# The output projection as seven block products instead of eight, with precomputed weight sums

## The chip, the core and the metric

The kernel runs on one core of a Trainium2 chip. The core has TensorE (PE, matrix products, with its weight loads shown apart as PEld), VectorE (DVE), ScalarE (ACT), GpSimd (POOL) and SyncE (SP, which here only issues DMAs). The engines run side by side, each through its own queue in order, and wait for one another through semaphores. The metric is the device time of one execution in microseconds, the median of several runs; each change is compared with the kernel before on the same chip.

## What is computed

One layer of a generator backbone: a modulated RMSNorm, a combined input projection, three groups of heads (a short convolution, neighbourhood attention, a conformer convolution), an output projection with a gated residual, and a last RMSNorm. Cut to what matters here, with x of 1024 rows and 1024 columns:

```python
mod = jax.nn.silu(c) @ w_ada[l] + b_ada[l]
shift, scale, gate = jnp.split(mod, 3, axis=-1)
...
ya = short_conv_branch(zl[0], zl[1], zl[2], zl[3], conv_sc[l])
yb = neighbourhood_attention(heads(zl[4]), heads(zl[5]), heads(zl[6]), kc, vc, rpb[l])
yb = yb * jax.nn.silu(zl[7])
yc = conformer_branch(zl[8], zl[9], zl[10], conv_cf[l], conv_cf_b[l], ln_cf_g[l], ln_cf_b[l])
y = jnp.concatenate([ya, yb, yc], axis=-1) @ w_out[l]
x = x + gate[:, None, :] * y
return rmsnorm(x, final_g)
```

Everything is float32. The product with `w_out` is 1024 x 1024 by 1024 x 1024.

## The kernel before

Matrix products are made in a rounded format: each float32 operand is split into a high part (a copy on ACT, line 129) and a low part (the difference, line 130, on DVE or on POOL), and a product is three matmuls: high by high, high by low, low by high. All y is kept transposed: eight channel tiles `y[0..7]` of 128 channels by 1024 positions; 0 and 1 come from the short convolution, 2 to 5 from attention, 6 and 7 from the conformer branch. Tiles 0 to 5 are written to DRAM (`yd`) when they are made and loaded again for the output projection.

The kernel first normalises and projects (up to about 150 us), then runs attention over four pairs of heads (`attend`, `attention`). There, for each block of 128 queries, PE makes scores (lines 596 and 597), DVE adds the bias and takes a minimum (601), ACT takes the exponential (604), POOL scales (606), PE transposes (615), ACT and DVE split (619, 620) and PE multiplies with the values (627). Other projections (329 to 331) and background work fill the gaps: a coroutine that is started with `spawn` emits a step whenever PE's estimated time has gone on by the gap that it yields, and `after_pe` puts an instruction behind the matmul emitted last, in the planner's order only. PE's order is the order in which the code emits; the orders of DVE, ACT, POOL and SP in this part are chosen by a planner when the program is built, and are then fixed queues.

The output stage follows attention (from line 1133). `load_wout(0)` loads and splits the left half of `w_out`, `load_y` loads and splits y; `cf_out` makes the last two y tiles with 96 projection matmuls; then come the products. `out_mm` makes one tile of 128 positions by 512 columns from all eight channel tiles, tile by tile, for the left half of the columns and then for the right: 8 tiles, 2 halves, 8 channels, 3 matmuls, that is 384 matmuls of 512 columns (the last tile's half in two pieces of 256). The first four tiles take channels 2 to 7 first and 0 and 1 behind the gate (`gate_rows`). For each tile and half, `out_part` (887) adds the gated result to the residual `xres` on DVE and sums squares on ACT (905); the left half is multiplied by the gate on DVE (894, 895), while for the right half the gate has been multiplied into the weights on POOL (865). `out_gain` (909) multiplies the first finished half by the last norm's gain on POOL, `out_mean` and `out_scale` work out the norm's factor on POOL (915 to 928) and scale on ACT (931) and DVE (933, 935), and each half is stored.

## Time and profile before

| | us |
|---|---|
| median of 3 runs (607.11 to 607.23) | 607.14 |
| the profiled execution | 607.07 |
| its span, from the first to the last instruction | 605.3 |
| first matmul of the output projection | 509.5 |
| start of its last matmul | 598.75 |
| end of DVE's last instruction | 601.55 |

The granted clock of TensorE was 0.997 of full speed in the mean. HBM traffic was 55.93 MB read and 14.29 MB written. Times in a profile are microseconds from the start of the span. A row of a timeline gives the start, the duration, the engine, the line, the operation, what it writes and reads, and in brackets the idle time before it and who ended it. A row of groups gives the count, the busy time, the mean duration in ns and the idle time before. Matmuls overlap one another: what a matmul costs is the distance between starts, not its own duration.

### The profile page before, as it was taken

What the parts mean: (1) busy time and instruction counts of PE and PEld (TensorE: products, weight loads), DVE (VectorE), ACT (ScalarE), POOL (GpSimd) and SP (SyncE); (2) the same over time, 40 slices, a digit from 0 to 9 for tenths busy, and PEclk for the clock granted to TensorE, in tenths of its full rate; (3) what the DMA queues carried; (4) which work ended last, traced back from release to release, by engine and by line L of the source; (5) the groups of instructions that cost most, each with busy time, mean ns of one, the idle gap of its engine ahead of it and who ended that gap; (6) DMA issues with size and microseconds to landing.
All of it is one profiled execution on the core that took longest, in us unless ns stands there. A gap on an engine that the chain in (4) does not pass through costs nothing.

```text
span 605.3 us, 8913 instructions
## 1 busy us (share of the span) xinstructions
PE 587.7 (97%) x3101; PEld 493.2 (81%) x3101; DVE 400.1 (66%) x681; ACT 245.9 (41%) x470; POOL 182.8 (30%) x194
## 2 busy tenths in 40 slices
PE   7799999999999999999999999999999999999995
PEld 4467888888898988888888988888887888888885
DVE  4466988665686699578897666936889347383222
ACT  2455721111355533454423555425655334024222
POOL 1031143000353212334112432114433460199311
PEclk9999999999999999999999999999999999999998
DMA  8992576975624026332145242172301464941122
GB/s 279 357 338 73 192 248 193 104 143 166 158 57 111 18 87 174 81 84 53 34 147 128 50 113 56 48 214 66 86 17 32 141 195 120 371 146 36 71 104 105
DMA packets 97170, 78.64 MB, mean 130 GB/s; under 512 B 26507, under 2 KB 80869, under 8 KB 96997
## 3 DMA queue, kind: packets, MB, share of 16 engines
q1 hardware_dynamic: 95397, 71.51, 42.6%
q10 hardware_dynamic: 1728, 6.55, 3.1%
q8 instruction: 25, 0.41, 0.3%
q14 instruction: 20, 0.16, 0.1%
HBM read 55.93 MB, written 14.29 MB: 116 GB/s over the span
## 4 chain that ended last, share of the span: by engine, by line
PE 86%; DVE 4%; ACT 3%; POOL 2%; issue 1%; DMA 1%; SPq 1%; POOLq 0%; DVEq 0%; ACTq 0%
PE ps_z L329 14%; PE ps_z L331 14%; PE ps_z L330 14%; PE po L627 5%; PE ps_t L615 5%; PE ps_f L878 5%; PE ps_f L879 5%; PE ps_f L877 5%; PE ps_s L596 3%; PE ps_z L419 3%; PE ps_z L421 3%; PE ps_z L420 3%; PE ps_s L597 2%; DMA wr<-in_w_in 1%; PE ps_h L279 1%
## 5 line engine op out<-in xcount | busy, mean ns | idle before, releaser
L329 PE MATMUL ps_z<-h,wh 128*128 128x512 f32 x384 | 151.1, 394 | 0.0
L331 PE MATMUL ps_z<-h,wl 128*128 128x512 f32 x384 | 150.3, 391 | 0.0
L330 PE MATMUL ps_z<-h,wh 128*128 128x512 f32 x384 | 149.8, 390 | 0.0
L130 POOL TENSOR_TENSOR wl<-wr,wh 128x512 fp32r<-128x512 f32 x44 | 61.4, 1399 | 165.4 <-ACT wh L129 162.0
L606 POOL TENSOR_SCALAR pr<-pr,sm 128x640 f32<-128x640 f32 (+1 forms) x64 | 56.6, 884 | 135.9 <-DVE sm L605 116.1
L331 PEld LDWEIGHTS ps_z<-h,wl 128*128 128x128 f32 x384 | 72.1, 188 | 16.1
L330 PEld LDWEIGHTS ps_z<-h,wh 128*128 128x128 f32 x384 | 72.1, 188 | 12.4
L329 PEld LDWEIGHTS ps_z<-h,wh 128*128 128x128 f32 x384 | 72.1, 188 | 12.1
L692 DVE SCALAR_TENSOR_TENSOR acc<-t,half_w,acc 128x1024 f32<-128x1024 f32 x60 | 80.6, 1343 | 1.2
L619 ACT ACTIVATE pw<-ps_t 128x640 fp32r<-128x640 f32 (+1 forms) x64 | 43.5, 680 | 86.8 <-PE ps_t L615 86.6
L601 DVE CUSTOM_DVE_ANT_0 ps_s<-ps_s,bt 128x640 f32<-128x640 f32 (+1 forms) x64 | 50.9, 796 | 27.1 <-PE ps_s L597 23.7
L620 DVE TENSOR_TENSOR pw<-ps_t,pw 128x640 fp32r<-128x640 f32 (+1 forms) x64 | 50.4, 788 | 15.8 <-ACT pw L619 15.5
L604 ACT ACTIVATE pr<-ps_s,mn 128x640 f32<-128x640 f32 (+1 forms) x64 | 49.1, 766 | 19.7 <-DVE mn L601 18.9
L878 PE MATMUL ps_f<-wol,y 128*128 128x512 f32 (+1 forms) x136 | 51.6, 379 | 0.0
L879 PE MATMUL ps_f<-woh,y 128*128 128x512 f32 (+1 forms) x136 | 51.6, 379 | 0.0
L877 PE MATMUL ps_f<-woh,y 128*128 128x512 f32 (+1 forms) x136 | 51.5, 379 | 0.0
L627 PE MATMUL po<-pw,vt 128*128 128x256 f32 x304 | 51.4, 298 | 0.0
L129 ACT ACTIVATE wh<-wr 128x512 fp32r<-128x512 f32 x46 | 29.0, 630 | 42.1 <-PE ps_z L330 21.7
L615 PE MATMUL ps_t<-ident,pr 128*128 128x128 f32 x304 | 43.6, 272 | 0.6 <-DVE sm L605 0.6
L596 PE MATMUL ps_s<-kt,qd 128*128 128x384 f32 (+1 forms) x128 | 39.8, 333 | 1.0 <-ACT pr L604 0.9
L627 PEld LDWEIGHTS po<-pw,vt 128*128 128x128 f32 x304 | 40.5, 190 | 0.3
L615 PEld LDWEIGHTS ps_t<-ident,pr 128*128 128x128 f32 x304 | 35.5, 141 | 2.1 <-issue 1.0
(169 smaller groups left out, 921.8 us busy)
## 6 DMA issues: line engine op xcount, KB each, us to landing
wr<-in_w_in SPq DMA_DIRECT2D x52, 256.0 KB
wa<-in_w_ada SPq DMA_DIRECT2D x16, 512.0 KB
qd<-qn SPq DMA_DIRECT2D x32, 256.0 KB
vd<-t SPq DMA_DIRECT2D x20, 256.0 KB
x_in<-in_x SPq DMA_DIRECT2D x8, 512.0 KB
t<-in_w_ada SPq DMA_DIRECT2D x16, 256.0 KB
vt<-vd SPq DMA_DIRECT2D x32, 128.0 KB
fraw<-in_w_out SPq DMA_DIRECT2D x8, 512.0 KB
```

Source lines behind the costliest of these rows:

```text
L130: i2 = (eng or nc.vector).tensor_tensor(out=lo, in0=src, in1=f32(hi), op=ALU.subtract)
L329: nc.tensor.matmul(ps, lhsT=wh, rhs=hh, start=(k == 0), stop=False)
L330: nc.tensor.matmul(ps, lhsT=wh, rhs=hl, start=False, stop=False)
L331: self.last = nc.tensor.matmul(ps, lhsT=wl, rhs=hh, start=False, stop=(k == KT - 1))
L596: nc.tensor.matmul(win, lhsT=q[:, b % 4], rhs=kwin, start=(i == 0), stop=(i == 1))
L606: nc.gpsimd.tensor_scalar(out=pr, in0=pr, scalar1=sm, scalar2=0.5, op0=ALU.mult, op1=ALU.mult)
L615: nc.tensor.transpose(out=pt[:, c * P:(c + 1) * P], in_=pr[:, c * P:(c + 1) * P], identity=self.ident)
L627: self.nc.tensor.matmul(po, lhsT=vt[:, vi, h], rhs=pw[:, c], start=(c == 0), stop=(c == n - 1))
L692: self.after_pe(nc.vector.scalar_tensor_tensor(out=acc, in0=u[:, t:t + T], scalar=self.half_w[:, 2 * t + ct:2 * t + ct + 1], in1=acc, op0= ...
L877: nc.tensor.matmul(ps, lhsT=yh, rhs=wh[:, ch], start=(first and i == 0), stop=False)
L878: nc.tensor.matmul(ps, lhsT=yh, rhs=wl[:, ch], start=False, stop=False)
L879: nc.tensor.matmul(ps, lhsT=yl, rhs=wh[:, ch], start=False, stop=(last and i == len(chs) - 1))
```

## The change

Write A for y (positions by channels) and B for `w_out`, each as 2 x 2 blocks of 512. The output blocks are made from seven block products. With S1 = A21 + A22, S2 = S1 - A11, S3 = A11 - A21, S4 = A12 - S2 and T1 = B12 - B11, T2 = B22 - T1, T3 = B22 - B12, T4 = T2 - B21, and with U = A11 B11 + S2 T2:

- left, first positions: A11 B11 + A12 B21
- right, first positions: U + S1 T1 + S4 B22
- left, second positions: U + S3 T3 - A22 T4
- right, second positions: U + S3 T3 + S1 T1

The sums T1 to T4 are made during attention by a new coroutine `out_weights` on POOL, split by ACT and POOL, in eight groups of [128 x 256] pieces, and written to DRAM (`wtd`, four tensors of 2.1 MB). The sums of y are made on DVE after `cf_out`; y is now kept unsplit and each A, S is split when it is needed (`y_parts`). Each product is `out_mm4`: four channel tiles outside, four position tiles inside, so four PSUM banks fill side by side and a quarter of the weights is free after every 12 matmuls; `load_wt` brings the next product's quarters into the same eight buffers. U and the sums on it are kept in SBUF tiles `fu`. Two sets of four PSUM banks take turns. The gate is now multiplied onto every result (`out_part` and two places beside it), partly on POOL (`G`); the weights no longer take it. The last product (A22 T4) goes tile by tile, the last tile in two pieces. `load_wout` and `y_tiles` go.

The diff, cut; lines of the old output loop are left out:

```diff
     def cf_out(self, ct):
         nc = self.nc
         acc, ch = self.acc_cf[ct], 6 + ct
-        yh, yl = self.y[ch] = self.y_tiles(ch, self.fp)
+        y = self.y[ch] = self.fp.tile([P, T], F32, name=f"y{ch}")
         def sink(half, ps):
             sl = slice(half * HALF, (half + 1) * HALF)
             sg = self.t2.tile([P, HALF], F32, name="t2", tag="t2")
             self.silu2(sg, ps)
-            nc.vector.scalar_tensor_tensor(out=sg, in0=acc[:, sl], scalar=0.25, in1=sg, op0=ALU.mult, op1=ALU.mult)
-            self.split(yh[:, sl], yl[:, sl], sg)
+            nc.vector.scalar_tensor_tensor(out=y[:, sl], in0=acc[:, sl], scalar=0.25, in1=sg, op0=ALU.mult, op1=ALU.mult)
...
+    def out_weights(self, pool, gap):
+        nc = self.nc
+        n = 256
+        for i in range(4):
+            for c in range(0, HALF, n):
+                def raw(k, half):
+                    t = pool.tile([P, n], F32, name="bg", bufs=5)
+                    nc.sync.dma_start(out=t, in_=self.a["w_out"][k * P:(k + 1) * P, half * HALF + c:half * HALF + c + n])
+                    return t
+                b11, b12, b21, b22 = raw(i, 0), raw(i, 1), raw(4 + i, 0), raw(4 + i, 1)
+                t1 = pool.tile([P, n], F32, name="bg", bufs=5)
+                yield gap
+                for name, out, x, y in (("T1", t1, b12, b11), ("T3", b12, b22, b12), ("T2", t1, b22, t1), ("T4", t1, t1, b21)):
+                    self.after_pe(nc.gpsimd.tensor_tensor(out=out, in0=x, in1=y, op=ALU.subtract))
+                    yield gap
+                    p = pool.tile([P, 2, n], F32R, name="bgp", bufs=2)
+                    i1, i2 = self.split(p[:, 0], p[:, 1], out, nc.gpsimd)
+                    self.after_pe(i1)
+                    self.after_pe(i2)
+                    yield gap
+                    nc.sync.dma_start(out=self.wtd[name][:, :, i, c:c + n], in_=f32(p))
+    def load_wt(self, name, pool):
+        w = [pool.tile([P, 2, HALF], F32R, name="wt", bufs=8) for _ in range(4)]
+        if name in self.wtd:
+            for i, t in enumerate(w):
+                self.nc.sync.dma_start(out=f32(t), in_=self.wtd[name][:, :, i])
+        return w
+    def load_b(self, pool, i, j, q, **kw):
+        src = self.a["w_out"][(4 * i + q) * P:(4 * i + q + 2) * P, j * HALF:(j + 1) * HALF]
+        t = pool.tile([P, 2, HALF], F32, **kw)
+        self.nc.sync.dma_start(out=t, in_=src.rearrange("(k p) n -> p k n", p=P))
+        return t
+    def split_b(self, w, raw, q):
+        for i in range(2):
+            self.split(w[q + i][:, 0], w[q + i][:, 1], raw[:, i], self.nc.gpsimd)
     def load_y(self, ch, pool):
-        raw = self.fr.tile([P, T], F32, name="fraw")
-        self.nc.sync.dma_start(out=raw, in_=self.yd[ch])
-        self.y[ch] = self.y_tiles(ch, pool)
-        self.split(*self.y[ch], raw)
+        self.y[ch] = pool.tile([P, T], F32, name=f"y{ch}")
+        self.nc.sync.dma_start(out=self.y[ch], in_=self.yd[ch])
...
+    def y_parts(self, pool, srcs):
+        r = []
+        for src in srcs:
+            t = pool.tile([P, 2, HALF], F32R, name="yc")
+            self.split(t[:, 0], t[:, 1], src)
+            r.append(t)
+        return r
...
+    def out_mm4(self, ps, y, w, first=True, skip=False):
+        for i in range(4):
+            for t in range(4):
+                self.out_mm(ps[t], i, t, y, w, first and i == 0, i == 3, skip=skip)
...
-    def out_part(self, tt, cs, j, ps, lp, eng):
+    def out_part(self, tt, cs, j, ps, lp, eng, op=ALU.add):
         nc = self.nc
         xt, ss = self.xres[tt]
         n = cs.stop - cs.start
         g = lp.tile([P, HALF], F32, name="fg", bufs=2)[:, 0:n]
-        if j == 0:
-            nc.vector.tensor_tensor(out=g, in0=ps[:, 0:n], in1=self.gate[:, cs], op=ALU.mult)
-            nc.vector.tensor_tensor(out=xt[:, cs], in0=g, in1=xt[:, cs], op=ALU.add)
-        else:
-
-            nc.vector.tensor_tensor(out=xt[:, cs], in0=ps[:, 0:n], in1=xt[:, cs], op=ALU.add)
+        nc.vector.tensor_tensor(out=g, in0=ps[:, 0:n], in1=self.gate[:, cs], op=ALU.mult)
+        nc.vector.tensor_tensor(out=xt[:, cs], in0=xt[:, cs], in1=g, op=op)
...
+        self.spawn(self.out_weights(r(self.pool("bg", 1, side="right")), 3.2), 4.0)
...
+            wt = e(self.pool("wt", 8, side="right"))
+            ya = e(self.pool("ya", 4, side="right"))
+            frs = ExitStack()
+            fr = frs.enter_context(self.pool("fr", 2, side="right"))
+            y, V, S, G = self.y, nc.vector, nc.scalar, nc.gpsimd
+            for ch in range(4):
+                self.load_y(ch, self.fp)
+            b11, b21 = (self.load_wt(n, wt) for n in ("B11", "B21"))
+            for i, b in enumerate((b11, b21)):
+                for q in (0, 2):
+                    self.split_b(b, self.load_b(fr, i, 0, q, name="fraw"), q)
+                if i == 0:
+                    a11 = self.y_parts(ya, [y[ch][:, 0:HALF] for ch in range(4)])
+            for ch in (4, 5):
                 self.load_y(ch, self.fp)
             self.run(self.cf_out(0), self.cf_out(1))
+            frs.close()
             inp.close()
             self.lp = lp = e(self.pool("lp", 1, side="left"))
...
+            ps_g = e(self.pool("ps_g", 4, PSUM, side="right"))
+            yc = e(self.pool("yc", 12, side="left"))
+            def banks(n=4, g=False):
+                pool, name, tag = (ps_g, "ps_g", "g") if g else (self.ps_f, "ps_f", "f")
+                return [pool.tile([P, HALF], F32, name=name, tag=tag) for _ in range(n)]
+            a12 = self.y_parts(yc, [y[4 + i][:, 0:HALF] for i in range(4)])
+            self.gate_load(lp, yc)
             self.fgam = lp.tile([P, D], F32, name="fgam")
             nc.scalar.dma_start(out=self.fgam, in_=self.a["final_g"].partition_broadcast(P))
...
             self.xres = []
...
+            sync, act = nc.sync.dma_start, nc.scalar.dma_start
+            h0, h1 = slice(0, HALF), slice(HALF, D)
+            u = []
+            ps = banks()
+            self.out_mm4(ps, a11, b11, skip=True)
+            for t in range(4):
+                u.append(lp.tile([P, HALF], F32, name=f"fu{t}"))
+                S.activation(out=u[t], in_=ps[t], func=AF.Copy)
+            for tt in range(4):
+                self.out_tile(tt, lp)
+            self.gate_rows(ps_g)
+            s1 = []
+            for i in range(4):
+                s = lp.tile([P, HALF], F32, name=f"fs{i}")
+                k1, k2 = y[i], y[4 + i]
+                V.tensor_tensor(out=s, in0=k1[:, h1], in1=k2[:, h1], op=ALU.add)
+                V.tensor_tensor(out=k1[:, h1], in0=k1[:, h0], in1=k1[:, h1], op=ALU.subtract)
+                V.tensor_tensor(out=k1[:, h0], in0=s, in1=k1[:, h0], op=ALU.subtract)
+                V.tensor_tensor(out=k2[:, h0], in0=k2[:, h0], in1=k1[:, h0], op=ALU.subtract)
+                s1.append(s)
+            t2 = self.load_wt("T2", wt)
+            s2 = self.y_parts(yc, [y[i][:, h0] for i in range(4)])
+            self.out_mm4(ps, a12, b21, False, skip=True)
+            t1 = self.load_wt("T1", wt)
+            s1 = self.y_parts(yc, s1)
+            raw = [self.load_b(yc, 1, 1, q, name="yc") for q in (0, 2)]
+            for t in range(4):
+                self.out_part(t, h0, 0, ps[t], lp, S)
+                self.out_mean(t, 0)
+                self.out_gain(t, h0)
+            ps = banks(g=True)
+            self.out_mm4(ps, s2, t2)
+            t3 = self.load_wt("T3", wt)
+            s3 = self.y_parts(yc, [y[i][:, h1] for i in range(4)])
+            for t in range(4):
+                V.tensor_tensor(out=u[t], in0=ps[t], in1=u[t], op=ALU.add)
+            for tt in range(4, 8):
+                self.out_tile(tt, lp)
+            ps = banks()
+            self.out_mm4(ps, s1, t1)
+            b22 = self.load_wt("B22", wt)
+            for q in (0, 2):
+                self.split_b(b22, raw[q // 2], q)
+            s4 = self.y_parts(yc, [y[4 + i][:, h0] for i in range(4)])
+            for t in range(4):
+                v = lp.tile([P, HALF], F32, name="fv", bufs=2)
+                V.tensor_tensor(out=v, in0=ps[t], in1=u[t], op=ALU.add)
+                V.tensor_tensor(out=v, in0=v, in1=self.gate[:, h1], op=ALU.mult)
+                for tt, eng in ((t + 4, V), (t, G)):
+                    x = self.xres[tt][0][:, h1]
+                    eng.tensor_tensor(out=x, in0=x, in1=v, op=ALU.add)
+            ps = banks(g=True)
+            self.out_mm4(ps, s3, t3)
+            t4 = self.load_wt("T4", wt)
+            a22 = self.y_parts(yc, [y[4 + i][:, h1] for i in range(4)])
+            for t in range(4):
+                V.tensor_tensor(out=u[t], in0=ps[t], in1=u[t], op=ALU.add)
+                self.out_part(t + 4, h1, 0, ps[t], lp, S)
+                self.out_mean(t + 4, 0)
+                G.tensor_tensor(out=u[t], in0=u[t], in1=self.gate[:, h0], op=ALU.mult)
+                x = self.xres[t + 4][0][:, h0]
+                G.tensor_tensor(out=x, in0=x, in1=u[t], op=ALU.add)
+                self.out_gain(t + 4, h1)
+            ps = banks()
+            self.out_mm4(ps, s4, b22)
+            for t in range(4):
+                self.out_part(t, h1, 1, ps[t], lp, S)
+                self.out_scale(t, 1, ((h0, S, sync), (h1, None, sync)))
+            ps = banks(3, True)
+            for t in range(3):
+                for i in range(4):
+                    self.out_mm(ps[t], i, t, a22, t4, i == 0, i == 3)
+                self.out_part(t + 4, h0, 1, ps[t], lp, S, ALU.subtract)
+                self.out_scale(t + 4, 1, ((h1, S, sync), (h0, None, sync)))
+            ps = banks(2)
+            q = [slice(c, c + 256) for c in (0, 256)]
+            for j in range(2):
+                for i in range(4):
+                    self.out_mm(ps[j], i, 3, a22, t4, i == 0, i == 3, 256 * j, 256 * j + 256)
+                self.out_part(7, q[j], 1 + j, ps[j], lp, (S, V)[j], ALU.subtract)
+                if j == 0:
+                    self.out_gain(7, q[0])
+                    self.out_mean(7, 1)
+            self.out_scale(7, 2, ((h1, S, act), (q[0], V, None), (q[1], None, sync)))
```

83 lines of the change are left out of this document (13 added, 70 removed).

## The prediction

> **What bounds the kernel now.** The page comes first, for the span, the busy shares and the chain of work that ended last.
>
> ```profile
> span 605.3 us, 8913 instructions
> PE 587.7 (97%) x3101; PEld 493.2 (81%) x3101; DVE 400.1 (66%) x681; ACT 245.9 (41%) x470; POOL 182.8 (30%) x194
> PE 86%; DVE 4%; ACT 3%; POOL 2%; issue 1%; DMA 1%; SPq 1%; POOLq 0%; DVEq 0%; ACTq 0%
> ```
>
> TensorE is busy for 97% of the span and carries 86% of the chain. The waits of PE from 150 to 480 us, which is all of attention, come next; these three rows are the whole answer.
>
> ```profile
> PE ps_z L734 <- DVE t L724: 1.0, 2, 0.7
> PE ps_s L596 <- ACT pr L604: 0.9, 3, 0.5
> PE ps_t L615 <- DVE sm L605: 0.6, 1, 0.6
> ```
>
> PE waits 2.5 us there in all. Then the table by stretches, over the output stage (columns: length, then busy time and count of PE, PEld, DVE, ACT, POOL; clock, DMA share, GB/s).
>
> ```profile
> 480.00:509.00 29.00, 29.00 (x129) 24.01 (x129) 14.51 (x15) 12.38 (x17) 12.51 (x6) 1.00 0.58 179
> 509.00:526.00 17.00, 17.00 (x77) 14.03 (x76) 6.34 (x9) 3.65 (x5) 0.00 (x0) 1.00 0.76 269
> 526.00:554.00 28.00, 28.00 (x125) 23.07 (x124) 18.65 (x16) 8.97 (x18) 25.43 (x14) 1.00 0.44 151
> 554.00:575.00 21.00, 21.00 (x92) 16.94 (x91) 5.72 (x8) 5.07 (x11) 11.15 (x17) 1.00 0.14 51
> 575.00:599.00 24.00, 24.00 (x128) 20.29 (x126) 6.12 (x9) 6.31 (x14) 4.25 (x10) 1.00 0.29 110
> ```
>
> From 509 to 599 PE never stops and DVE works 18.65 of 28 us at its worst and a quarter of the time later (6.12 of 24). So this stage is PE's: a matmul less is a matmul's time less, as long as the other engines keep up. Whether they do is the whole question.
>
> **What is removed.** The view of tile ps_f gives the matmuls of the output projection, the PE timeline the start of the last one.
>
> ```profile
> L877 PE MATMUL ps_f<-woh,y x136: 276/389/398, 509.5 to 598.5; 128*128 128x512 f32 x120, 128*128 128x256 f32 x16
> 525.89 1.09 PE L843 MATMUL ps_g<-ghl,ones_r 128*128 128x512 f32 x4
> 526.82 0.39 PE L877 MATMUL ps_f<-woh,y 128*128 128x512 f32 x1
> 598.75 0.28 PE L879 MATMUL ps_f<-woh,y 128*128 128x256 f32 x1
> ```
>
> Three lines of 120 full and 16 half matmuls are 384 full ones. They take 598.75 - 509.5 less the 0.93 us of the gate matmuls (525.89 to 526.82): 88.3 us, or 0.230 us each. Seven products of 4 x 4 x 3 are 336. PE saves 48 x 0.230 = **11.0 us**, and its last matmul would start near 587.7. The multiplication by the gate of the second weight half on POOL (L865) goes too; it hid behind PE.
>
> **What is added after cf_out.** The DVE and POOL timelines have the prices, and what the two do to each other.
>
> ```profile
> 510.91 0.58 ACT L390 ACTIVATE t<-ps_z 128x512 f32<-128x512 f32 x1
> 512.36 0.69 DVE L802 SCALAR_TENSOR_TENSOR t<-acc,t 128x512 f32<-128x512 f32 x1
> 528.39 0.69 DVE L894 TENSOR_TENSOR fg<-ps_f,gate 128x512 f32<-128x512 f32 x1 [0.55 <-PE ps_f L879]
> 531.66 2.17 DVE L895 TENSOR_TENSOR xres<-fg,xres 128x512 f32<-128x512 f32 x1
> 533.76 0.68 DVE L894 TENSOR_TENSOR fg<-ps_f,gate 128x512 f32<-128x512 f32 x1
> 540.16 1.34 DVE L895 TENSOR_TENSOR xres<-fg,xres 128x512 f32<-128x512 f32 x1
> 555.07 0.69 DVE L895 TENSOR_TENSOR xres<-fg,xres 128x512 f32<-128x512 f32 x1
> 595.99 0.75 DVE L935 SCALAR_TENSOR_TENSOR xres<-xres,fss,fgam 128x512 f32<-128x512 f32 x1 [1.85 <-POOL fss L928]
> 596.66 0.42 DVE L898 TENSOR_TENSOR xres<-ps_f,xres 128x256 f32<-128x256 f32 x1
> 601.07 0.48 DVE L935 SCALAR_TENSOR_TENSOR xres<-xres,fss,fgam 128x256 f32<-128x256 f32 x1
> 528.06 5.22 POOL L865 TENSOR_TENSOR fraw<-fraw,gate 128x1024 f32<-128x1024 f32 x2 [32.36 <-DVE gate L845]
> 533.25 5.73 POOL L130 TENSOR_TENSOR wol<-fraw,woh 128x1024 fp32r<-128x1024 f32 x2
> 539.66 1.29 POOL L909 TENSOR_TENSOR xres<-xres,fgam 128x512 f32<-128x512 f32 x1
> L895 DVE TENSOR_TENSOR xres<-fg,xres 128x512 f32<-128x512 f32 x8 | 13.6, 1697 | 0.3
> ```
>
> An independent DVE instruction starts about 0.08 us before its forerunner's record ends (595.99 + 0.75 against 596.66), so a full [128 x 512] one costs 0.61 us of DVE and a scaling 0.67. DVE can begin the new work when cf_out's last values are made; the last of them was ready at 512.36 + 0.69. Its tanh (L390) started at 510.91 though its matmuls ended by 509.5, because ACT copied for a split that is now gone; 1.4 us earlier, and with the overlap of 0.08, is 511.5. From the diff, DVE then has, full width: two SBUF inputs: 16 sums of y, 24 splits (a12, s2, s1, s3, s4, a22), 4 residual additions after the second product, 8 after the fourth, 4 + 4 + 3 after the last three, 63 in all; one PSUM input: 2 for the gate and 4 + 4 + 4 + 8 + 4 + 3 evictions, 29; 7 scalings; and about 2.9 us on the last tile's halves. That is 92 x 0.61 + 7 x 0.67 + 2.9 = **63.7 us**. Before, DVE was busy 18.65 + 5.72 + 6.12 = 30.5 us from 526 to 599.
>
> To this come the waits for POOL. L895, two SBUF inputs, takes 0.69 us when POOL rests (555.07), 1.34 when it meets a 1.29 us POOL instruction (540.16) and 2.17 when it meets 2.6 us ones. It ends half a microsecond after POOL's instruction does (531.66 + 2.17 = 533.83; POOL's pair ended at 533.28), while L894, which reads PSUM, stays at 0.69. So the two take turns: a DVE instruction with two SBUF inputs waits out POOL's. The row of 540.16 prices a meeting with a 512-wide one at 1.34 - 0.69 = 0.65 us, and POOL now has little else than those.
>
> The Trainium skill (SBUF — State Buffer, section "SBUF: two separate sides") calls this port pair an exclusive lock that the first comer holds for its whole instruction, with no sharing of bandwidth; the ends quoted above agree. By sharing instead, each meeting would cost what the group's mean shows, 1.70 - 0.69 = 1.01 us, and the waits worked out below would come to 33 us, not 21.
>
> How many meetings? These rows price POOL's small steps.
>
> ```profile
> 563.50 0.27 POOL L925 TENSOR_SCALAR fss<-fss 128x1 f32<-128x1 f32 x1
> 563.85 0.56 POOL L928 TENSOR_TENSOR fss<-fss,mhalf 128x1 f32<-128x1 f32 x1
> 597.76 0.74 POOL L909 TENSOR_TENSOR xres<-xres,fgam 128x256 f32<-128x256 f32 x1 [1.80 <-ACT fsq L905]
> ```
>
> POOL after 511.5: about 3 splits left of B21, 4 of B22, 8 gains (0.74 us of them narrow), 12 sums into u and the residual, near 27 x 1.29 + 0.74 = 35.6 us, and some 9 us of small steps (8 x 0.83 and the means): 45 us. Over a stage of 95 us that is 0.47 of the time. DVE's 63 + 7 instructions with two SBUF inputs then wait 70 x 0.47 x 0.65 = **21 us** (none if the two always miss each other; 70 x 0.65 = 45 if every one meets one, as most of L895's eight do with their mean of 1.70). Bunching speaks for more: in the fifth product POOL gets four 512-wide instructions for one tile of evictions less one, 3 x 1.29 + 0.3 = 4.2 us a tile, 17 us in all against a product of 48 x 0.230 = 11.0 us. Everything it does for the last norms (L925, L928) stands behind that backlog.
>
> ```profile
> 508.93 0.68 DVE L391 SCALAR_TENSOR_TENSOR t<-t,ps_z 128x512 f32<-128x512 f32 x1
> 509.65 0.69 DVE L802 SCALAR_TENSOR_TENSOR t<-acc,t 128x512 f32<-128x512 f32 x1
> 573.64 0.75 DVE L935 SCALAR_TENSOR_TENSOR xres<-xres,fss,fgam 128x512 f32<-128x512 f32 x1 [1.85 <-POOL fss L928]
> 515.25 9.80 ACTq L883 DMA_DIRECT2D xres<-in_x  x4
> ```
>
> Idle time of DVE: some 27 pairs in which it reads its own last result (509.65 follows 508.93 + 0.68 by 0.04 where independent ones overlap 0.08, so 0.12 each, 3 us), and waits at the end for POOL's small steps behind the backlog. Before, such a wait was 1.85 us a tile. I take **8 us**, between 4 (one wait) and 14 (six).
>
> ACT has room: 28 copies for splits, 8 for B21 and B22, 4 of u at near 0.6 us, and the norms as before, some 40 us of 90. But its queue also issues the residual loads, and four took 9.80 us to issue. The copies of u, which free the banks for the second product, and the split copies stand behind them. That delay is 0 to 9.8 us of PE; I take 0 for the end, since DVE is already late there. DMA adds 8.4 MB of loads (four sums of 2.1 MB) to the 12.5 MB of the last four rows of the table; less 2 for the weights no longer read, 19 MB in 80 us is 240 GB/s, under the 269 that 509:526 shows. Each quarter of a weight block is freed as its twelve matmuls are done, so a sum has a whole product, 11 us, for its 2.1 MB: 190 GB/s. I cost it at nothing; late, it would be PE's wait.
>
> ```profile
> 597.17 0.42 ACT L905 ACTIVATE fsq<-xres 128x256 f32<-128x256 f32 x1 [0.45 <-DVE xres L898]
> L606 POOL TENSOR_SCALAR pr<-pr,sm x64: 696/803/2102, 160.4 to 469.5; 128x640 f32<-128x640 f32 x48, 128x512 f32<-128x512 f32 x16
> ```
>
> **What is added during attention.** 64 POOL instructions and 32 ACT copies of 256 columns, in 72 steps of 3.2 us: 230 of the 309 us between the first and the last L606. DVE's instructions on scores read PSUM and, like L894, don't mind POOL; the convolution on DVE does, but nothing on PE waits for it there. POOL's softmax scaling (L606) and ACT's exponential stand behind them. PE waited 0.9 us in total for L604 and 0.6 for L605, so the room is thin for ACT: 32 copies of 0.42 us (L905's narrow form) are 13 us if each hits, 0 if none. By the waits row of L604, 3 of 64 blocks waited, so few will: I take **1 us**.
>
> **The sum**, in the profiled execution's time: 511.5 + 63.7 + 21 + 8 + 1 = 605.2 for DVE's last instruction, against 601.07 + 0.48 = 601.55 before. From there to the span's end, the last store, 605.3 - 601.55 = 3.75 us; to the profiled execution's own 607.07 (the median is 607.14), another 1.8. So 610.8, say **611**. PE would be done near 589, and the end is DVE's and POOL's: 11 us are won on PE and some 15 given back behind its last matmul.
>
> **Rivals.** *DVE and POOL keep up, PE stays the bound.* The point is W, waits plus idle: up to 25 us (601.55 - 511.5 - 63.7 - 1) the kernel is not slower, and my 29 is not far off; that the orders of DVE and POOL are a planner's, unseen here, speaks for it as much as against. If W is under some 16, PE's end decides: 587.7 + 2.8 as before, one more instruction per part and a scaling or two late, 2, is 592.5; with 3.75 and 1.8, **598**. Chance 0.26, spread from 598 to 606.
> *Port bound, as summed*: 0.62, own range 606 to 619.
> *Attention stalls on top.* In-order POOL waits for a raw weight load, L606 waits behind it, PE stops; 8 groups at the 0.5 us of L596's longest wait and a third of ACT's 13 us are 8 us more, **619**. The slack says rarely: 0.12.
> *That it doesn't do what it says*: the 48 matmuls go by the code. Sums not ready in time would show as PE waiting for T2; 80 us lie between. I give it nothing of its own.
>
> **Range and chances.** 600 to 619 leaves out the fastest part of the first rival and the worst of the last. A difference under 0.2% (1.2 us) is about what a measurement here can't tell from none. Faster 0.25, the same 0.08, slower 0.67.
>
> **What would show it.** Right: PE's last matmul at 587 to 592 and ten or more microseconds from it to the last DVE instruction; L895's successor and the splits at 1 us or more in the mean; POOL over half busy from 565 on, with L928 behind the gains. Wrong: DVE idle in the last two products (then the waits are too dear here), or PE waiting in attention (the third rival), or for a T load.

## The result, and the profile after

The changed kernel takes **625.8 us** (median of 4 runs, 625.5 to 627.2) beside 607.2 (4 runs, 607.1 to 607.8): a ratio of 1.0313, 95% interval 1.0301 to 1.0325. The direction is the one predicted, but the loss is 18.6 us and not 4. The profiled execution took 627.2 us; its page begins so (span, busy times, POOL's busy tenths, then the chain that ended last):

```profile
span 625.2 us, 9212 instructions
...
PE 582.7 (93%) x3041; PEld 485.7 (78%) x3041; DVE 439.3 (70%) x744; ACT 264.6 (42%) x528; POOL 241.8 (39%) x270
...
POOL 1031232001546334555444455345433440055863
...
PE 58%; DVE 12%; SPq 9%; DMA 6%; POOL 6%; ACT 4%; issue 4%; DVEq 0%; ACTq 0%; POOLq 0%
```

PE's share of the chain has fallen from 86% to 58%. SP's queue and DMAs, 1% each before, now hold 9% and 6% of it: a first hint at where to look. The waits of PE from 150 to 480 us, three rows of 2.5 us before, are now four; the three longest:

```profile
PE ps_s L596 <- ACT pr L604: 4.8, 5, 3.0
PE ps_s L597 <- DVE kt L380: 3.0, 2, 1.9
PE ps_z L734 <- DVE t L724: 1.6, 2, 1.1
```

The view of tile ps_f, the last row of PE's timeline, and the table by stretches over the output stage (columns as before):

```profile
L911 PE MATMUL ps_f<-wt,yc x72: 279/394/398, 523.5 to 601.8; 128*128 128x512 f32 x64, 128*128 128x256 f32 x8
```

```profile
602.00 0.28 PE L913 MATMUL ps_f<-wt,yc 128*128 128x256 f32 x1
```

```profile
526.00:554.00 28.00, 27.53 (x122) 22.33 (x121) 25.42 (x41) 12.36 (x26) 4.15 (x4) 1.00 0.99 362
554.00:575.00 21.00, 21.00 (x93) 17.25 (x92) 16.02 (x18) 7.14 (x12) 11.80 (x11) 1.00 0.47 168
575.00:599.00 24.00, 24.00 (x106) 19.69 (x105) 18.42 (x25) 4.34 (x12) 19.15 (x16) 1.00 0.22 70
599.00:626.00 27.00, 3.28 (x26) 3.00 (x25) 13.83 (x24) 9.90 (x20) 10.79 (x20) 0.64 0.42 156
```

The 19.9 us of span (605.3 to 625.2) split at two marks, the first output matmul and the last one:

| | before | after | difference |
|---|---|---|---|
| span's start to the first output matmul | 509.5 | 523.5 | +14.0 |
| first to last output matmul | 89.2 | 78.5 | -10.7 |
| last output matmul to the span's end | 6.55 | 23.2 | +16.6 |

So PE gets its 11 us. Attention (all that stands ahead of the first output matmul) loses 14 and the tail 16.6.

**The tail.** DVE's timeline at the end of the sixth product, and POOL's beside it:

```profile
592.80 0.68 DVE L933 TENSOR_TENSOR fg<-ps_f,gate 128x512 f32<-128x512 f32 x1
602.54 0.78 DVE L971 SCALAR_TENSOR_TENSOR xres<-xres,fss,fgam 128x512 f32<-128x512 f32 x1 [9.07 <-POOL fss L964]
...
604.44 0.68 DVE L934 TENSOR_TENSOR xres<-xres,fg 128x512 f32<-128x512 f32 x1
```

```profile
595.64 1.29 POOL L1267 TENSOR_TENSOR fu<-fu,gate 128x512 f32<-128x512 f32 x1
...
600.32 1.29 POOL L945 TENSOR_TENSOR xres<-xres,fgam 128x512 f32<-128x512 f32 x1
601.60 0.27 POOL L961 TENSOR_SCALAR fss<-fss 128x1 f32<-128x1 f32 x1
601.95 0.56 POOL L964 TENSOR_TENSOR fss<-fss,mhalf 128x1 f32<-128x1 f32 x1
```

DVE stands 9.07 us at one scaling (L971) that needs a norm, with evictions that need none (L934, L933) queued behind it. POOL has the norm late because the fifth product's gates, additions and gains keep it busy until 601.6.

**Attention.** The stretch from 188 us, first ACT's rows and SP's queue in the changed kernel, then SP's in the kernel before:

```profile
190.31 0.63 ACT L129 ACTIVATE wh<-wr 128x512 fp32r<-128x512 f32 x1 [5.91 <-DMA wr<-in_w_in]
190.85 0.69 ACT L619 ACTIVATE pw<-ps_t 128x640 fp32r<-128x640 f32 x1
191.43 0.68 ACT L604 ACTIVATE pr<-ps_s,mn 128x512 f32<-128x512 f32 x1
```

```profile
175.95 8.24 SPq L509 DMA_DIRECT2D bt<-u  x11
184.29 0.56 SPq L874 DMA_DIRECT2D wT<-bgp  x1
184.89 1.57 SPq L860 DMA_DIRECT2D bg<-in_w_out  x3
186.51 0.43 SPq L310 DMA_DIRECT2D wr<-in_w_in  x1
```

```profile
175.37 5.18 SPq L509 DMA_DIRECT2D bt<-u  x7
180.65 1.58 SPq L310 DMA_DIRECT2D wr<-in_w_in  x2
182.32 1.37 SPq L364 DMA_DIRECT2D qd<-qn  x2
```

Each DMA in these rows holds SP for 0.4 to 0.8 us (the column behind the start is the time of the group's issues). With the background's loads and stores among them, the load of the next raw weight block (wr) is issued at 186.51 in place of 180.65. ACT, in order, stands 5.91 us at the copy of that block, and behind this copy are the softmax copies and the exponential on which PE waits. Over all of attention (150 to 510 us) the row of this copy, before and after, reads (x count, busy, mean ns, idle before it and its causes):

```profile
L129 ACT ACTIVATE wh<-wr 128x512 fp32r<-128x512 f32 x34 | 21.4, 630 | 23.3 <-PE ps_z L330 21.7 <-PE ps_z L331 0.8 <-ACT pr L604 0.6
```

```profile
L129 ACT ACTIVATE wh<-wr 128x512 fp32r<-128x512 f32 x33 | 20.8, 629 | 32.7 <-PE ps_z L330 18.2 <-DMA wr<-in_w_in 14.6
```

ACT waits 14.6 us for loads that it never waited for. That is a reading, not a proof: POOL's and ACT's extra work came in with the same change.

### The profile page after: what moved, and what is told of

Its sections match the earlier page's. It is cut to its first block, busy times and chain, and to the rows that moved or that the text cites. A ratio compares the mean times of both kernels' runs of the same rounds, so it can differ in the third digit from the quotient of the medians.

```text
span 625.2 us, 9212 instructions
## 1 busy us (share of the span) xinstructions
PE 582.7 (93%) x3041; PEld 485.7 (78%) x3041; DVE 439.3 (70%) x744; ACT 264.6 (42%) x528; POOL 241.8 (39%) x270
## 3 DMA queue, kind: packets, MB, share of 16 engines
q10 hardware_dynamic: 1872, 6.55, 2.8%
## 4 chain that ended last, share of the span: by engine, by line
PE 58%; DVE 12%; SPq 9%; DMA 6%; POOL 6%; ACT 4%; issue 4%; DVEq 0%; ACTq 0%; POOLq 0%
PE ps_z L329 9%; PE ps_z L331 9%; PE ps_z L330 9%; SPq L509 4%; PE ps_t L615 3%; PE po L627 3%; DMA wr<-in_w_in 3%; DVE acc L692 3%; PE ps_z L419 3%; PE ps_z L421 3%; PE ps_z L420 3%; PE ps_s L596 3%; PE ps_s L597 2%; SPq L364 2%; DMA yc<-gd 1%
## 5 line engine op out<-in xcount | busy, mean ns | idle before, releaser
L130 POOL TENSOR_TENSOR wl<-wr,wh 128x512 fp32r<-128x512 f32 x44 | 60.1, 1370 | 142.8 <-ACT wh L129 136.2
L692 DVE SCALAR_TENSOR_TENSOR acc<-t,half_w,acc 128x1024 f32<-128x1024 f32 x60 | 82.2, 1369 | 1.2
L330 PEld LDWEIGHTS ps_z<-h,wh 128*128 128x128 f32 x384 | 73.0, 190 | 12.7
L329 PEld LDWEIGHTS ps_z<-h,wh 128*128 128x128 f32 x384 | 73.0, 190 | 12.3
L619 ACT ACTIVATE pw<-ps_t 128x640 fp32r<-128x640 f32 (+1 forms) x64 | 43.4, 679 | 74.2 <-PE ps_t L615 74.1
L604 ACT ACTIVATE pr<-ps_s,mn 128x640 f32<-128x640 f32 (+1 forms) x64 | 49.0, 766 | 18.8 <-DVE mn L601 17.9
L597 PE MATMUL ps_s<-kt,qd 128*128 128x256 f32 x128 | 35.7, 284 | 3.0 <-DVE kt L380 3.0
L130 POOL TENSOR_TENSOR bgp<-bg,bgp 128x256 fp32r<-128x256 f32 x32 | 28.0, 874 | 19.2 <-ACT bgp L129 19.2
L596 PEld LDWEIGHTS ps_s<-kt,qd 128*128 128x128 f32 x128 | 24.1, 188 | 11.9 <-ACT pr L604 9.9
```

Of the source, the lines that this page charges most:

```text
L130: i2 = (eng or nc.vector).tensor_tensor(out=lo, in0=src, in1=f32(hi), op=ALU.subtract)
L329: nc.tensor.matmul(ps, lhsT=wh, rhs=hh, start=(k == 0), stop=False)
L330: nc.tensor.matmul(ps, lhsT=wh, rhs=hl, start=False, stop=False)
L596: nc.tensor.matmul(win, lhsT=q[:, b % 4], rhs=kwin, start=(i == 0), stop=(i == 1))
L604: nc.scalar.activation(out=pr, in_=s, func=AF.Exp, scale=-1.0, bias=mn, accum_out=sm)
L692: self.after_pe(nc.vector.scalar_tensor_tensor(out=acc, in0=u[:, t:t + T], scalar=self.half_w[:, 2 * t + ct:2 * t + ct + 1], in1=acc, op0= ...
```

## The experiments

The times of before and after are the medians of four executions, that of m1 the median of ten; every other is one execution, beside 607.0 to 607.5 us of the kernel before on the same chip. "First" is the start of the first output matmul, "DVE" the end of DVE's last instruction, in the profiled execution; all three in us. How far equal stages differ from run to run can be read from the table too: the seven rows that have the changed kernel's output stage, and no long stop at the gate rows, have 96.9 to 97.6 in the last column; the five that have its attention (after, f1, f2, f12, k3) have 523.5 to 525.2 under "first".

| run | time | first | DVE | DVE less first |
|---|---|---|---|---|
| before | 607.2 | 509.5 | 601.6 | 92.0 |
| after | 625.8 | 523.5 | 621.2 | 97.6 |
| e1_no_bg | 613.2 | 510.0 | 607.6 | 97.6 |
| e2_bg_compute | 620.6 | 517.9 | 614.8 | 96.9 |
| e3_bg_dma | 626.5 | 523.9 | 621.0 | 97.0 |
| e4_bg_act | 634.5 | 531.1 | 628.0 | 96.9 |
| k1_bg_pool | 633.0 | 528.6 | 625.9 | 97.2 |
| g1_merged | 624.2 | 511.7 | 618.3 | 106.6 |
| g2_merged_early | 623.0 | 520.2 | 617.0 | 96.9 |
| f1_scales_last | 623.0 | 524.0 | 616.7 | 92.7 |
| f2_gate_on_dve | 625.5 | 525.2 | 619.0 | 93.8 |
| f12_both | 621.5 | 524.1 | 613.8 | 89.7 |
| k3_no_pool_ops | 616.6 | 523.5 | 609.9 | 86.3 |
| h1_all | 620.8 | 513.0 | 615.1 | 102.1 |
| j1_g2_f1_f2 | 613.0 | 516.7 | 606.3 | 89.6 |
| j2_g2_f3_f2 | 615.0 | 520.1 | 608.7 | 88.6 |
| k2_j1_pool | 609.7 | 512.1 | 601.8 | 89.7 |
| m1_j2_pool | 609.1 | 512.7 | 601.8 | 89.1 |

### What in the background costs the 14 us

Four runs on the changed kernel: without the background, with its sums alone, with its DMAs alone, and whole with its DMAs on ACT's queue.

```diff
@@ e1 @@
-        self.spawn(self.out_weights(r(self.pool("bg", 1, side="right")), 3.2), 4.0)
@@ e1, e2, e3: load_wt @@
-                self.nc.sync.dma_start(out=f32(t), in_=self.wtd[name][:, :, i])
+                self.nc.sync.dma_start(out=f32(t), in_=self.gd[:, i % 2])
@@ e2: out_weights @@
+                if i == 0 and c == 0:
+                    b11, b12, b21, b22 = raw(i, 0), raw(i, 1), raw(4 + i, 0), raw(4 + i, 1)
...
-                    nc.sync.dma_start(out=self.wtd[name][:, :, i, c:c + n], in_=f32(p))
@@ e3: out_weights @@
-                    self.after_pe(nc.gpsimd.tensor_tensor(out=out, in0=x, in1=y, op=ALU.subtract))
...
-                    i1, i2 = self.split(p[:, 0], p[:, 1], out, nc.gpsimd)
...
+                        nc.sync.dma_start(out=self.wtd[name][:, k, i, c:c + n], in_=v)
@@ e4: out_weights, the store and in the same way the load @@
-                    nc.sync.dma_start(out=self.wtd[name][:, :, i, c:c + n], in_=f32(p))
+                    nc.scalar.dma_start(out=self.wtd[name][:, :, i, c:c + n], in_=f32(p))
```

> Leaves out the weight sums of attention altogether; the seven products read quarters of the same size from another tensor, so the output stage does all its work on other data. In the changed kernel the first output matmul came at 523.5 us instead of 509.5, and PE stood still 11.3 us in gaps of over 0.4 us after 100 us, against 2.1 before. If all of that comes from the background work of attention (both theories below), the first output matmul is back at 509.5 to 510.5 and the time is 625.8 - 14 = 611 to 613. If it stays later than 513, something else in the change moves attention. The time from the first output matmul to the end (625.2 - 523.5 = 101.7 us) should stay within 1 us, if the output stage's cost doesn't come from attention.

> Keeps the 64 subtractions on POOL and the 32 copies on ACT during attention, but loads the weight pieces only once and stores nothing; the products read other data of the same size. Theory Q (queue): the 64 extra DMAs on SP stand ahead of the loads of queries (L364) and projection weights (L310), whose data PE then waits for; so without them the first output matmul is at 510 to 512 and the time 612 to 614. Theory W (work): POOL's and ACT's extra instructions stand ahead of the softmax scaling, the exponential and the key copies; so the delay stays, first output matmul at 520 to 524, time 622 to 626.

> Keeps the 32 loads of weight pieces and stores on SP during attention (stores cut in two halves, 64 of half the size, straight from the loaded pieces), but none of the subtractions and copies; the products read other data of the same size. Theory Q: most of the delay stays, first output matmul at 517 to 524, time 619 to 626. Theory W: 510 to 512, time 612 to 614. Here no store waits for POOL, so if Q's delay comes from SP waiting on the stores and not from the issues themselves, this falls between, 512 to 516.

> The changed kernel with the background's 64 DMAs issued from ACT's queue instead of SP's, all else the same. Theory Q: the loads of queries and weights are on time again, first output matmul at 510 to 515 (ACT pays some for the issues and for waiting on POOL before stores), time 612 to 617. Theory W: no better than 523.5, or worse, since ACT, which makes the exponential, gets more to do: 524 to 530, time 626 to 632.

Without the background the first output matmul is where it was before, give or take 0.5 us, and the tail keeps its whole length: **the two losses are separate**. The DMAs alone cost 14.4 us, as theory Q had it; but they are 96 in that run and not 64, since its stores are cut in two. There SP's queue and ACT's read:

```profile
184.56 1.92 SPq L870 DMA_DIRECT2D wT<-bg  x4
186.53 1.89 SPq L860 DMA_DIRECT2D bg<-in_w_out  x4
188.51 1.37 SPq L364 DMA_DIRECT2D qd<-qn  x2
189.93 2.10 SPq L310 DMA_DIRECT2D wr<-in_w_in  x2
```

```profile
194.25 0.63 ACT L129 ACTIVATE wh<-wr 128x512 fp32r<-128x512 f32 x1 [7.47 <-DMA wr<-in_w_in]
```

Eight background issues, 3.8 us, ahead of the loads, and ACT stands at the same copy for 7.47 us. But the sums alone, with four loads in all and no store, cost 8.4 us too: 517.9 lies between what Q had (510 to 512) and what W had (520 to 524), and neither is the whole. Most of it is one place (POOL's and ACT's timelines of that run):

```profile
162.43 0.72 POOL L868 TENSOR_TENSOR bg<-bg 128x256 f32<-128x256 f32 x1 [4.42 <-DMA bg<-in_w_out]
```

```profile
163.19 0.42 ACT L129 ACTIVATE bgp<-bg 128x256 fp32r<-128x256 f32 x1 [6.05 <-POOL bg L868]
163.51 0.67 ACT L604 ACTIVATE pr<-ps_s,mn 128x512 f32<-128x512 f32 x1
```

POOL waits for a raw piece, ACT's copy for POOL, and the exponential stands behind the copy. It is the prediction's third rival, with one more link. 8.4 and 14.4 are more than 14.0 together, so the parts don't add: a likely reason, not tested, is that whoever stands already does not lose the time a second time. From ACT's queue the loss grows to 21.6 us, worse than even W had (524 to 530), in many waits of at most 1.3 us: now ACT issues the DMAs, and waits for POOL's halves ahead of the stores.

Next, the same sums and bytes in half as many DMAs, each twice as large (the changed kernel has 32 loads and 32 stores, g1 16 and 16; the expectation's 64 and 64, and its quarter, are miscounted), with three more steps between a load and its use and steps of 2.4 in place of 3.2; the same with steps of 1.9; and the background of the changed kernel on POOL's queue.

```diff
@@ g1, g2: out_weights @@
-                    t = pool.tile([P, n], F32, name="bg", bufs=5)
+                t = pool.tile([P, 2, 2, n], F32, name="bg", bufs=1)
+                for j in range(2):
...
+                    nc.sync.dma_start(out=t[:, j], in_=src)
...
+                for k in range(2):
+                    for _ in range(3):
+                        yield gap
...
+                    nc.sync.dma_start(out=out, in_=f32(p.rearrange("p a l x -> p (a l) x")))
@@ k1: out_weights, the store and in the same way the load @@
-                    nc.sync.dma_start(out=self.wtd[name][:, :, i, c:c + n], in_=f32(p))
+                    nc.gpsimd.dma_start(out=self.wtd[name][:, :, i, c:c + n], in_=f32(p))
```

> The background sums of the weights are made with 16 loads of two pieces each and 16 stores of two sums each in place of 64 loads and 64 stores of one, with more time between a load and its use; sums, splits and bytes are the same. Theory Q (the attention loses its 14 us where qd, wr and the other loads of SP's queue are issued behind background DMAs): with a quarter of the DMAs the first output matmul is at 511-515 us (523.53 in after) and the time 612-618 us. Theory W (POOL's and ACT's extra work delays the attention's own): the first output matmul stays at 517 us or later, as in the run with that work and no stores (517.93), and the time at 620 us or more.

> The merged background DMAs with less time between the steps of the background (1.9 in place of 2.4). In the run with 2.4 the first output matmul came at 511.74, but the last background store was issued at 498.8, the loads of the raw weights behind it at 501.8, and PE stood 7.5 us at the gate rows at 522-531. Theory Q+ (that gap is the late end of the background): the background ends by 450-470, the gap falls below 1.5 us, the first output matmul stays by 516 and the time is 614-618 us. If the gap is a matter of the merged layout of the stores (shorter or more crowded reads in the output stage), it stays at 5 us or more and the time at 622-625 us.

> The changed kernel with the 64 background DMAs issued from POOL's queue; same bytes, sums and splits, and SP's queue holds only what it held before the change. Theory Q (the loads of qd and wr are issued late because they stand behind background DMAs in SP's queue): the 6 us at 188-198 and the 3 us at 249-254 go, the first output matmul is at 511-517 us (523.53 in after, 531.11 from ACT's queue), the time 612-619 us. Theory L (the background's traffic slows the loads wherever it is issued): the first output matmul stays at 520 us or more. Theory W (POOL's and ACT's extra work): it stays at 517 us or more, as in the run with that work alone, and more if issuing costs POOL time.

With the DMAs merged, attention loses 2.2 us in place of 14.0, as theory Q had it. The time hardly moved all the same (624.2, where Q had 612 to 618): the background's last store was issued at 498.8 us, and PE stood at the gate rows,

```profile
PE ps_g L843 <- DMA yc<-gd: 7.0, 2, 5.7
```

because the chain of waits now leads from the raw weights' loads (502 us and 512 us, behind the background) over their splits and DVE's sums of y to this load. With shorter steps this gap is gone, but the first output matmul is at 520.2, not by 516: ACT's copies of the sums wait 8.3 us for POOL's subtractions, and the weight copies 6.9 us for wr. So the gap was the late end, as Q+ had it; its 516 fails. That the shorter step is the cause of these waits is not shown: j1 below has the same background and 516.7.

From POOL's queue, with SP as free as before the change, theory Q fails as it stood: 528.6. The loss at 188 us does go (from 150 to 240 us PE's longest stall is 0.80 us), but POOL pays for the issues with its own time, 42.1 us of these two rows (the profile counts DMAs from this queue as software_dynamic, those of SP as hardware_dynamic, so the queue is not all that changed):

```profile
L874 POOL DMA_DIRECT2D wT<-bgp x32 | 22.6, 707 | 9.0 <-POOL bgp L130 8.9
L860 POOL DMA_DIRECT2D bg<-in_w_out x32 | 19.5, 610 | 52.6 <-PE ps_z L421 47.5 <-POOL bg L867 5.0
```

PE's longest wait, 4.13 us, is then at 250 us: the weight copy waits for wr again, this time with no background DMA in SP's queue; the reload waited for an earlier wr to land and for POOL to free its buffer. So what costs is not SP's queue as such. **The loads of wr had little slack: work put into SP's queue (e3) or into POOL's (k1), through which they, their buffers and their copies pass, makes them late.** The bytes don't set the loss, and with that theory L is out: the same 12.6 MB cost 2.2 us in g1 and 21.6 in e4. Whether the number of issues does, or the time between a load and its use, is not separated, since g1 changed both; and g2, with g1's 32 issues and only shorter steps, lost 10.7. Merged and on POOL's queue (k2, m1 below) the background costs 2.6 and 3.2 us.

### What sets the tail

```diff
@@ f1 @@
-                self.out_scale(t, 1, ((h0, S, sync), (h1, None, sync)))
...
-                self.out_scale(t + 4, 1, ((h1, S, sync), (h0, None, sync)))
+                behind = self.out_part(t + 4, h0, 1, ps[t], lp, S, ALU.subtract)
+            for t in range(4):
+                self.out_scale(t, 1, ((h0, S, sync), (h1, None, sync)), behind)
+            for t in range(3):
+                self.out_scale(t + 4, 1, ((h1, S, sync), (h0, None, sync)), behind)
@@ f2 @@
-                G.tensor_tensor(out=u[t], in0=u[t], in1=self.gate[:, h0], op=ALU.mult)
+                V.tensor_tensor(out=u[t], in0=u[t], in1=self.gate[:, h0], op=ALU.mult)
...
-                G.tensor_tensor(out=x, in0=x, in1=u[t], op=ALU.add)
+                V.tensor_tensor(out=x, in0=x, in1=u[t], op=ALU.add)
@@ k3, on f1 and f2 @@
+        if tt == 7:
             self.nc.gpsimd.tensor_tensor(out=xt[:, cs], in0=xt[:, cs], in1=self.fgam[:, cs], op=ALU.mult)
...
-                for tt, eng in ((t + 4, V), (t, G)):
+                for tt, eng in ((t + 4, V),):
```

`behind` makes the scalings of DVE and ACT follow the given eviction and square in their queues. f12_both is f1 and f2 together.

> The last scalings of seven of the eight row tiles are put behind the last eviction (DVE) and the last square (ACT); the work of every engine is the same, only its order changes. Theory O (the tail is an order: DVE stands 9.07 us, from 593.48 to 602.54, at the first of these scalings, which waits for POOL's norm, while evictions that need no norm are queued behind it): this stall is filled, DVE's own work ends 5 to 9 us earlier and the time falls from 625.8 to 616-621 us. Theory D (the sum of DVE's work and of its waits at the shared port sets the end, in whatever order): within 2 us of 625.8. Theory B (POOL's backlog, busy to 601.6, and the scalings and 4 MB of stores behind it set the end): within 2 us too, as the norms come no earlier.

> The fifth product's eight multiplications by the gate and additions into the sum (two for each of four tiles) go from POOL to DVE. Theory B (POOL's backlog of 582.0 to 601.6 sets the end): POOL is free about 8 x 1.35 = 11 us earlier, the norms of the last tiles come 6 to 11 us earlier and the time falls to 616-620 us. Theory D (DVE's own work sets the end): DVE has 8 x 0.61 = 5 us more and loses about as much in waits at the port: 624-631 us. Theory O (the stall of DVE behind a norm): the stall shrinks by what POOL is earlier, as in B, less DVE's 5 us: 620-625 us.

> Both edits of the tail on the changed kernel: the last scalings behind the last eviction, and the fifth product's gate and addition on DVE. Alone they gave 623.02 and 625.52 us; from the first output matmul to DVE's end 92.7 and 93.8 us in place of 97.6. If order (O) and POOL's backlog (B) are two losses, the gains add and DVE ends 88-90 us after the first output matmul, 617-621 us in all. If they are two descriptions of one stall, this run is no better than the better of the two: 92-94 us, 622-626 us.

Attention varies by 1.7 us among these (523.5 to 525.2 to the first output matmul), so the last column of the table is what to read. Order alone takes 4.9 us off, POOL's relief alone 3.8, both 7.9: nearly the sum, so these are **two losses**. In the time each gave less than expected: f1 took 623.0 us where O had 616 to 621, f12 621.5 where the sum had 617 to 621, and f2's 625.5 lies in the range of D, not of B or O. What speaks against D there is the 93.8, and that DVE's waits for the last norms fell from 13.7 to 5.3 us. In f1 POOL is still busy with the backlog to 603.2, and seven norms follow 1.2 us apart. In f12 DVE's waits for the last norms have shrunk from 13.7 us to 0.7, and DVE is busy for 81.0 of its 89.7 us (the expectation below has 80.3). That is work, not waiting, unless the port is in it. The last run of this group leaves out part of POOL's work; by its edit these are 11 operations (seven gains and four additions) and not the 18 that its expectation counts:

> The run with both edits of the tail, and 18 of POOL's tensor operations of the output stage left out: the gains (the product with final_g) of seven tiles' first halves and the fourth product's additions into tiles 0 to 3. DVE's work is unchanged. Theory P (DVE's long operations are waits for POOL at the port that they share): DVE's 11 us of excess over its usual durations falls below 3 us, its busy time from 80.3 to 69-72 us, and it ends 79-84 us after the first output matmul in place of 89.7. If the excess is DVE's own (PSUM reads, ordering), its busy time stays at 78 us or more.

DVE's busy time falls from 81.0 to 74.1 us; two of the groups that have two SBUF inputs, first in f12 and then in k3 (the lines differ by one):

```profile
L130 DVE TENSOR_TENSOR yc<-y,yc 128x512 fp32r<-128x512 f32 x20 | 17.3, 900 | 3.6 <-ACT yc L129 3.5
L1262 DVE TENSOR_TENSOR xres<-xres,fv 128x512 f32<-128x512 f32 x4 | 6.0, 1498 | 0.0
L933 DVE TENSOR_TENSOR fg<-ps_f,gate 128x512 f32<-128x512 f32 x8 | 5.2, 682 | 1.3 <-PE ps_f L913 1.3
```

```profile
L130 DVE TENSOR_TENSOR yc<-y,yc 128x512 fp32r<-128x512 f32 x20 | 15.3, 790 | 4.9 <-ACT yc L129 4.7
L1263 DVE TENSOR_TENSOR xres<-xres,fv 128x512 f32<-128x512 f32 x4 | 3.6, 910 | 0.0
L933 DVE TENSOR_TENSOR fg<-ps_f,gate 128x512 f32<-128x512 f32 x8 | 5.2, 685 | 1.4 <-PE ps_f L913 1.4
```

The PSUM reader (L933) is untouched, the others shorten: the long operations are waits for POOL, some 7 us here. (POOL waits too: in the changed kernel's fifth product, the five of its eight L1267 and L1269 that met DVE's L934 took 1.63 to 1.83 us, the other three 1.29 to 1.30.) The expectation was 69 to 72 busy and an end 79 to 84 us after the first output matmul; both are missed by about 2 us (POOL keeps four splits of B22 and the small steps, and DVE waits more for ACT's copies).

### Both together

h1 is g1 with f2; j1 is g2 with f1 and f2; j2 has each last scaling one tile behind the evictions; k2 is j1, and m1 is j2, with the background on POOL's queue.

```diff
@@ j2, m1: one scaling in each step of the last product @@
                 behind = self.out_part(t + 4, h0, 1, ps[t], lp, S, ALU.subtract)
+                self.out_scale(t, 1, ((h0, S, sync), (h1, None, sync)), behind)
...
+                    self.out_scale(4, 1, ((h1, S, sync), (h0, None, sync)), behind)
...
+            for t in (5, 6):
+                self.out_scale(t, 1, ((h1, S, sync), (h0, None, sync)), behind)
```

> The merged background DMAs and the fifth product's gate on DVE together. If the losses in the attention and in the tail are independent (the run without the background kept a tail of 22.9 us), the gains of the two single runs add: with theories Q and B 602-610 us, with Q and D 612-620, with W and D no better than 620.

> All three: merged and earlier background, last scalings last, gate on DVE. If attention and tail are independent: first output matmul 511-514, DVE's end 88-90 us later, 601-605, and a time of 605-610 us, on either side of before's 607. If they are not (engines that are early run into the next limit, as in the run with the merged background and the gate on DVE, 620.78): 612 us or more.

> As the run before, but the last scalings stand one tile behind the evictions of the last product (one scaling behind each) in place of all behind the last. With POOL free of the backlog the norms of the first four tiles should be ready when their turn comes: then the scalings and stores fill DVE's waits for the last product and the end is 2-4 us earlier than with all scalings last. If DVE stands at the norms again, it is 2-4 us later.

> The merged and earlier background with its 32 DMAs on POOL's queue, and both edits of the tail. With the first output matmul at 511-513 us, and the 94.4 us from there to the end that the run with both edits and the merged background had (516.69 to 611.08), the span is 605-607 and the time 607-609 us: as fast as before. If the stalls at 160 and 245 us come from POOL's and ACT's own work, it is 611-614 us.

> The merged background on POOL's queue, the fifth product's gate on DVE, and the last scalings one tile behind the last product's evictions. First output matmul 511-514 us as in the run with the same background (512.08), and 93.1 us from there to the end as in the run with the same output stage (520.08 to 613.14): span 604-607, time 606-609 us. DVE is busy in about 81 of its 89 us there, so nothing of PE's 11 us can be left: if the account is right, this version is within 0.4% of before (607.2) and not faster by more than that.

The tail is 88.6 to 89.7 us wherever both edits are in and PE does not stand at the gate rows. The scalings one tile behind gave 1.0 us (j2 against j1) and 0.6 (m1 against k2), not the 2 to 4 expected, and no more than the 0.7 us by which equal output stages differ. h1 missed (620.8, where Q and B had 602 to 610): with g1's late background PE stands 5.8 us at the gate rows again. What missed in j1 (613.0, where 605 to 610 was expected) and in j2 is attention: 516.7 and 520.1, from one and the same background. In the traces of g2 (520.2), j1 and j2 all five engines run the same instructions in the same order up to 470 us, so these 3.5 us are a difference from run to run; most of it arises where POOL waits for the first raw piece, 3.11 us in j1, 5.70 in g2 and 3.95 in j2. With the 32 DMAs on POOL's queue the first output matmul is at 512.1 and 512.7, and k2's time of 609.7 lies just outside its 607 to 609.

The last version takes 609.1 us (10 runs, 608.1 to 611.6) beside 607.2 (13 runs, 606.5 to 607.9): 1.0039, interval 1.0024 to 1.0054. It has little left of the two losses (3.2 us in attention, none in the tail, whose 89.1 us are below before's 92.0), and is still not faster than before, but 0.4% slower. Its table by stretches says why:

```profile
563.00:590.00 27.00, 27.00 (x127) 22.44 (x126) 27.00 (x37) 5.28 (x15) 11.97 (x15) 1.00 0.24 72
590.00:608.00 18.00, 1.29 (x11) 1.08 (x10) 11.11 (x21) 8.21 (x18) 9.10 (x14) 0.59 0.63 234
```

DVE is busy 27.00 of 27.00 us under the last products and 11.1 of 18 behind them. Its last instruction ends at 601.8 us, where it ended before the change.

## Why the prediction was right or wrong

**PE's saving**: right. 10.7 us where 11.0 was worked out, and 19.2 us from the last matmul to DVE's last instruction, where "ten or more" was named as the sign. POOL was over half busy from 554 to 599 us, about as said. The other sign, splits and residual additions at 1 us or more in the mean, failed (0.86 and 0.79), and two signs of being wrong came: PE waiting in attention, and DVE idle in the last two products.

**The term that failed: attention, "I take 1 us".** It was 14.0. The step's sentence that the room was thin only for ACT, with 32 copies of 0.42 us, priced the work that the background adds to POOL and ACT and left its 64 DMAs out of the account: they stand in SP's queue ahead of wr and qd. The bound of 13 us from above was for copies that hit; it was passed, by another way. e1, which leaves the background out, takes 613.2 us, near the 610 that the sum gives without this term. The waits of before (0.9 us for L604) were taken as a measure of slack, and they can't be: a wait of zero says that something was in time, not by how much. The same holds of the third rival: its mechanism, a raw load that POOL waits for, is what e2 shows, at one place of 3.6 us and not eight of 0.5, and the rival missed the queue in front of the loads.

**The sum for DVE**: near in total by luck, wrong in its parts. Shifted by the 14 us, DVE could begin at 525.5 and ended at 621.15, 95.7 us later, where 63.7 + 21 + 8 = 92.7 was the sum. These rows of DVE by shape, from 523.5 us on, show the parts:

```profile
L130 DVE TENSOR_TENSOR yc<-y,yc 128x512 fp32r<-128x512 f32 x20 | 16.6, 856 | 4.3 <-ACT yc L129 4.3
L934 DVE TENSOR_TENSOR xres<-xres,fg 128x512 f32<-128x512 f32 x15 | 11.5, 790 | 0.0
L1258 DVE TENSOR_TENSOR xres<-xres,fv 128x512 f32<-128x512 f32 x4 | 6.0, 1498 | 0.0
L971 DVE SCALAR_TENSOR_TENSOR xres<-xres,fss,fgam 128x512 f32<-128x512 f32 x7 | 5.7, 821 | 13.0 <-POOL fss L964 13.0
...
L1255 DVE TENSOR_TENSOR fv<-fv,gate 128x512 f32<-128x512 f32 x4 | 3.8, 954 | 0.0
```

Over 0.69 us each (0.75 for L971), these groups are 20 x 0.17 + 15 x 0.10 + 4 x 0.81 + 7 x 0.07 + 4 x 0.26 = 9.7 us too long: the **waits at the port were 10 us, not 21**. The product 70 x 0.47 took it that POOL and DVE are busy independently of each other. In fact POOL was busy for 8.4 of the 9.07 us in which DVE stood at the norm, and could not meet it there. The rule of the Trainium skill (SBUF — State Buffer, section "SBUF: two separate sides"), one lock for the port of both, agrees with k3, whose shortened groups are those with two SBUF inputs; it says nothing on how often the two meet, and that was the error. **Idle time was 21.5 us, not 8**: 13.7 for norms where "one wait" to "six" were to make 4 to 14 with everything else, 4.3 for ACT's copies, and some 3 for PE. So one term was 11 us too high and the other 13.5 too low, and the errors cancelled. That POOL's backlog in the fifth product would hold up the norms stands in the prediction; what it missed is that a fixed order puts DVE's evictions behind such a norm, and so turns POOL's lateness into DVE's.

**The rivals.** That DVE and POOL keep up did not happen, and the bound named for it (waits plus idle up to 25 us) was passed: 10 + 21.5. It is not the order alone: with order and backlog mended, waits and idle time are still 16 to 20 us (7 to 11 at the port, 8.7 idle in f12), beside the 8 x 0.61 = 4.9 us of work that DVE took over from POOL, and in m1 DVE ends at 601.8 us, where it did before. That sums come in time held: PE waited for no T block.

**The range** ended at 619 because the attention term was bounded by ACT's copies. With 14 in place of 1 the sum is 611 + 13 = 624, against 625.5 to 627.2 measured.

## What to carry to other kernels

Work put "in the background" costs first by its place in in-order queues, and DMA issues count as work: before adding any, list for each queue (SP's too) what stands behind the new entries, and measure how early that was before, not how long somebody waited for it. Half as many DMAs with more time before their use took the loss here from 14.0 to 2.2 us; which of the two did it stays open. When a faster method takes time from the bound engine and gives additions to another, add up the other's whole stage, and look in its order for an instruction that waits for a third engine with ready work behind it.
